# A hybrid decoder step on one core: new owners for the four PSUM banks of its chunked recurrence

## The chip, the core and the metric

The kernel runs on one core of a Trainium2 chip. The metric is device time in microseconds (us) of one execution; the figure to beat is the median of three timed runs. Engines are called PE or TensorE (matmul; PEld is its weight load), DVE or VectorE, ACT or ScalarE, POOL or GpSimd, and SP, whose queue issues most of the DMAs.

## What is computed

One inference step of a two-layer decoder trunk in float32, for a prompt of 1024 positions and for 8 sample sequences of 8 positions that share the weights. Layer 0 has a Conformer convolution mixer, layer 1 an RWKV-7 time mixer; each layer then has cross-attention to 256 memory tokens and a squared-ReLU MLP. The part that the change touches is the recurrence of layer 1, 16 heads with a 64 x 64 state each:

```python
def step(s, inp):
    rt, wt, kt, vt, at, bt = inp
    sa = jnp.einsum('bhvk,bhk->bhv', s, at)
    s = s * wt[:, :, None, :] + sa[..., None] * bt[:, :, None, :] + vt[..., None] * kt[:, :, None, :]
    yt = jnp.einsum('bhvk,bhk->bhv', s, rt)
    return s, yt
...
y, s = wkv7_scan(rh, decay, kh, vh, -kk, kk * ah, s0)
y = standardize(y, LNX_EPS).reshape(bsz, t, d) * lnx_g + lnx_b
y = (y + bonus.reshape(bsz, t, d)).astype(h.dtype)
out = (y * g) @ rw_w_o
```

## The kernel before

The positions are cut into two parts. Stream A works on part 0 (512 prompt positions), stream B on part 1 (512 prompt positions and the 64 sample positions). Each stream goes through all stages of both layers. A planner (`pace`) interleaves the two in program order: each stage is a generator that yields planned microseconds, and the stream whose planned clock is behind goes next. From that program order, with priorities, a scheduler at build time fixes the order on every engine and queue and puts in the semaphore waits; on the chip each engine and queue works strictly in its fixed order. The scan has its priority raised by 1000 places (`SCAN_AHEAD`).

Large products are made of three matmuls on high and low parts (lines 142 to 144); each weight tile is loaded to a raw buffer (four of them, line 120), cast on ScalarE (line 96) and split on VectorE or GpSimd (line 97).

The recurrence (`scan`) works on chunks of 64 positions, 8 columns of 128 partitions (two heads in each). Stream A scans chunks 0 to 7 beside B's projections; B then scans the samples (chunk `None`) and chunks 8 to 15 beside A's output projection, attention and MLP of layer 1. Projections leave r, k, v, the decay, a and g of every position in a DRAM scratch, in slots 0 to 5. Of a chunk three generators exist, and `together` gives each a turn in rotation, for three neighbouring chunks at once:

- `prep` loads five slots into `ld` (one buffer; eight DMAs at line 1146) and works on them elementwise (lines 1159 to 1196, `ar` and `bk` on GpSimd at 1183 to 1192); then products: sums (1201), the pair products of `ar` and `bk` (1217) with masks into `at`, `Aak`, `Aq` (1220 to 1222), v transposed into `UV` (1228, 1230), `bk` transposed into `BK` (1238), `AV` (1244, 1246), and last the bonus `bon`, which reads v in `ld` (1249, 1251).
- `inverse` inverts the chunk's triangular matrices: small blocks on VectorE, then four hops on TensorE (1320, 1326, 1335, 1345), each followed by an evacuation.
- `rest` has `step` and `finish`. `step` is the recurrence itself: `pz` from the state S (1374), y's part from S (1378), Z (1381), U (1386) and its two copies into `UV` (1387, 1388), the state's product (1393) and y's part from `UV` (1396), and the new S (1398, 1399). `finish` copies y (1488) and normalises it: sum (1445), centred y (1446), square (1449), sum (1450), Ln (1452), Exp (1453), five GpSimd instructions, and the store.

The scan has four of the eight PSUM banks; the other stream has the other four. In the kernel before they are called `pp` (two buffers in rotation), `pz` and `py`:

| bank | who uses it, for each chunk |
|---|---|
| `pp`, two | ten turns of `prep`, four hops of `inverse` (tag `iv`), U of `step` |
| `pz` | the two products of `step` that are added to `AV` and to S |
| `py` | y from its first product to its copy, then both norm sums |

Of the kernel before, what the change touches and what calls it, by code (L numbers as in the profile page):

```python
# [171 lines left out]
def body(tc, nc, es, a, o):  # L172
# [556 lines left out]
    def projections(s, ctx, part, h):  # L729
# [136 lines left out]
        def project(slot, after, *sides):  # L866


            for m0, k in ((0, 2), (2, 1), (3, 1), (4, 1), (5, 1), (6, 2)):
                wts = weights.take(k)  # L870
                for tt in tiles:
                    t0, n = tt
                    for m, wt in enumerate(wts, m0):
                        ps = s.bank()
                        s.prod(ps[:, :n], wide(wt, h, tt))
                        t = s.small("st")
                        nc.scalar.copy(t[:, :n], ps[:, :n])
                        store(t, m, slot, t0, n)
                        yield cost(n)
                        for side in sides:  # L880
                            yield next(side, 0)
                    if m0 == 6 and after is not None:
                        yield from mix(after, tt)
# [200 lines left out]
PE_PAIRS = (4, 3)  # L1084
BUF = dict(w=5, bon=2, at=2, ar=2, Aq=2, UV=2, AV=2, BK=2, pcs=3)


def scan(tc, nc, a, o, s, ph, kept, env):
# [9 lines left out]
    def bank(tag):  # L1098
        if tag == "iv":
            tag = "pp"  # L1100
        return sps.tile([P, 512], F32, tag=tag, name="p_" + tag, bufs=2 if tag == "pp" else 1)

    bones = con_tile(cn, "bones")
# [28 lines left out]
    def v3(t):  # L1132
        return t.rearrange("p (c t) -> p c t", c=8)
# [14 lines left out]
    def prep(chunk):  # L1148

        sam = chunk is None  # L1150
        kind = "_s" if sam else "_p"
        ld = new([P, 5, 512], "ld")
        load(ld, chunk, slice(0, 5))
        r, k, v, ws, ag = (ld[:, i] for i in range(5))
        ar = new([P, 8, 2, 64], "ar")
# [104 lines left out]
    def invert(at, tt, deep):  # L1260
# [48 lines left out]
        def iv():  # L1309
            return bank("iv")[:, :256].rearrange("p (i t) -> p i t", i=8)  # L1310

# [55 lines left out]

    def step(w, py, S):

        UV = w["UV"]  # L1370
        pz = v3(bank("pz"))
        for i in range(8):
            for h, s in heads:
                nc.tensor.matmul(pz[s, i], lhsT=w["ar"][s, i, 0], rhs=S[s, i], start=True, stop=True)

        for i in range(8):
            for h, s in heads:
                nc.tensor.matmul(py[s, i * 64:i * 64 + 64], lhsT=S[s, i], rhs=w["ar"][s, i, 1], start=(i == 0),
                                 stop=False)
        Z = new([P, 8, 64], "Z8")  # L1380
        nc.vector.tensor_add(Z, pz, w["AV"])
        yield
        pu = v3(bank("pp"))
        for i in range(8):
            for h, s in heads:
                nc.tensor.matmul(pu[s, i], lhsT=w["tt"][s, i], rhs=Z[s, i], start=True, stop=True)
        nc.vector.tensor_copy(UV[:64, :, 0], pu[:64])
        nc.scalar.copy(UV[:64, :, 1], pu[64:])
        yield
        pz = v3(bank("pz"))  # L1390
        for i in range(8):
            for h, s in heads:
                nc.tensor.matmul(pz[s, i], lhsT=w["BK"][:, i, h], rhs=UV[:, i, h], start=True, stop=True)
        for i in range(8):
            for h, s in heads:
                nc.tensor.matmul(py[s, i * 64:i * 64 + 64], lhsT=UV[:, i, h], rhs=w["Aq"][:, i, h], start=False,
                                 stop=(i == 7))
        nc.vector.tensor_add(S, pz, S)
        nc.vector.tensor_tensor(S, S, w["pcs"].unsqueeze(2).broadcast_to([P, 8, 64]), MUL)

    def step_samples(w, y, q):
# [7 lines left out]

        py = bank("py").rearrange("p (c i t) -> p c i t", c=4, i=2)  # L1410
        for g, c in enumerate(range(8)[cs]):
# [30 lines left out]

    def finish(w, y, py):
        chunk = w["chunk"]
        nc.tensor.matmul(py, lhsT=bones, rhs=y, start=True, stop=True)
        nc.vector.scalar_tensor_tensor(out=y, in0=py, scalar=-1.0 / 64, in1=y, op0=MUL, op1=ADD)
        yield
        rs = w512("rs")
        nc.scalar.activation(rs, y, AF.Square, scale=1.0 / 8)
        nc.tensor.matmul(py, lhsT=bones, rhs=rs, start=True, stop=True)  # L1450
        yield
# [17 lines left out]
    def rest(w):  # L1469

        chunk = w["chunk"]
        y = w512("y")
        if chunk is None:
            for i in range(2):
                yield from step_samples(w, y, i)
                yield
            py = bank("py")
        else:
            py = bank("py")
            if chunk == 0:  # L1480
                state[0] = states.tile([P, 8, 64], F32, tag="S", name="S")
                nc.gpsimd.memset(state[0], 0.0)
            S = state[0]
            yield from step(w, py, S)
            yield
            if chunk == 15:
                nc.sync.dma_start(out=o["wkv_p"].rearrange("m p v -> p m v"), in_=S)
            nc.scalar.copy(y, py)
        yield
        yield from finish(w, y, py)  # L1490
        yield
# [179 lines left out]
```

## Time and profile before

| | |
|---|---|
| timed runs | median 3887.41 us of 3 (3883.94 to 3888.81) |
| the profiled execution | 3875.96 us, span 3874.2 us, mean granted clock 0.955 |
| TensorE busy | 3627.8 us, 94% of the span |
| VectorE, ScalarE, GpSimd busy | 61%, 42%, 17% |
| scan of stream A | about 1740 to 2215 us of the span |
| scan of stream B | about 2375 to 2940 us of the span |

The profile has one execution. Busy times are unions of an engine's instructions. In a list of waits, "PE X <- DVE Y" says that TensorE stood idle before X until VectorE ended Y. The clock of TensorE is given as a share of full speed. A float32 matmul of this kernel shows as two rows of the trace, so 16 matmuls are x32. A row with "<-issue" has no releaser that the profile shows.

### The profile page before, as it was taken

To read this page: it belongs to the slowest core of one execution; us is meant where nothing else is said; L and a number is where in the kernel's file an instruction comes from. 1 tells how busy PE (TensorE), PEld (TensorE's weight loads), DVE (VectorE), ACT (ScalarE), POOL (GpSimd) and SP (SyncE) were. 2 spreads that over 40 slices of the span, in tenths; PEclk is the share of its full clock that TensorE was granted. 3 is DMA by queue.
4 is the path that set the end of the run, shared out by engine and by line. 5 is a ranking of instruction groups with operands and counts; after the bars stand their busy time and mean duration, and the time that the engine had idled before them with its cause. 6 is when DMAs were issued, how large, how long until landed. Compare 5 with 4: busy or idle time off the path is not lost. (4 is left out here: it accounts for less than half of the span.)

```text
span 3874.2 us, 75595 instructions
## 1 busy us (share of the span) xinstructions
PE 3627.8 (94%) x30906; PEld 3366.4 (87%) x30906; DVE 2353.9 (61%) x4479; ACT 1616.1 (42%) x3180; POOL 656.7 (17%) x704
## 2 busy tenths in 40 slices
PE   8989979999999999999899888979899999989998
PEld 7767769999999999999678688757789999989998
DVE  7889974646554653438767526587875536563334
ACT  3223253445433454443556634344444336432222
POOL 0010031024101100012221200232222015101110
PEclk9989989999999999999799899879899999999998
DMA  6424223335422344453245385323224336422221
GB/s 223 131 58 127 81 63 111 99 123 175 146 87 85 124 157 157 156 147 91 83 140 152 93 272 158 98 67 82 67 75 142 112 103 193 144 77 82 82 82 63
DMA packets 330827, 456.01 MB, mean 118 GB/s; under 512 B 153072, under 2 KB 245488, under 8 KB 330480
## 3 DMA queue, kind: packets, MB, share of 16 engines
q1 hardware_dynamic: 302832, 424.42, 35.9%
q10 hardware_dynamic: 27648, 26.75, 2.0%
q8 instruction: 243, 3.98, 0.4%
q14 instruction: 104, 0.85, 0.1%
HBM read 369.11 MB, written 73.49 MB: 114 GB/s over the span
## 5 line engine op out<-in xcount | busy, mean ns | idle before, releaser
L97 DVE TENSOR_TENSOR wt<-raw,wt 128x1024 fp32r<-128x1024 f32 x447 | 569.6, 1277 | 490.2 <-ACT wt L96 483.2
L96 ACT CAST wt<-raw 128x1024 fp32r<-128x1024 f32 x488 | 508.2, 1046 | 489.3 <-PE B_d L144 254.0
L142 PE MATMUL B_d<-hAB,wt 128*128 128x288 f32 (+1 forms) x2240 | 671.1, 302 | 12.6 <-ACT wt L96 5.2
L142 PE MATMUL A_d<-hAA,wt 128*128 128x256 f32 x2240 | 639.2, 288 | 32.8 <-ACT wt L96 16.7
L143 PE MATMUL B_d<-hBB,wt 128*128 128x288 f32 (+1 forms) x2240 | 668.5, 299 | 0.2
L144 PE MATMUL B_d<-hAB,wt 128*128 128x288 f32 (+1 forms) x2240 | 664.8, 298 | 0.5 <-DVE wt L97 0.3
L143 PE MATMUL A_d<-hBA,wt 128*128 128x256 f32 x2240 | 640.1, 287 | 4.2 <-DVE hBA L97 4.1
L144 PE MATMUL A_d<-hAA,wt 128*128 128x256 f32 x2240 | 632.5, 285 | 4.8 <-DVE wt L97 2.6
L142 PEld LDWEIGHTS A_d<-hAA,wt 128*128 128x128 f32 x2240 | 428.6, 192 | 49.5 <-ACT wt L96 20.9
L142 PEld LDWEIGHTS B_d<-hAB,wt 128*128 128x128 f32 x2240 | 424.1, 190 | 22.3 <-ACT hAB L96 7.5
L143 PEld LDWEIGHTS A_d<-hBA,wt 128*128 128x128 f32 x2240 | 429.9, 192 | 14.1 <-DVE hBA L97 5.9
L144 PEld LDWEIGHTS A_d<-hAA,wt 128*128 128x128 f32 x2240 | 427.7, 192 | 10.7 <-DVE wt L97 3.4
L143 PEld LDWEIGHTS B_d<-hBB,wt 128*128 128x128 f32 x2240 | 425.8, 190 | 5.2 <-DVE hBB L97 1.5
L144 PEld LDWEIGHTS B_d<-hAB,wt 128*128 128x128 f32 x2240 | 425.3, 190 | 3.2 <-issue 1.7
L711 POOL TENSOR_TENSOR t_sg<-t_ev 128x256 f32<-128x256 f32 (+1 forms) x256 | 185.0, 723 | 1427.8 <-ACT t_ev L709 1329.9
L142 PE MATMUL B_d<-u,wt 128*128 128x288 f32 x1024 | 304.2, 299 | 0.0
L144 PE MATMUL B_d<-u,wt 128*128 128x288 f32 x1024 | 302.2, 298 | 0.0
L143 PE MATMUL B_d<-u,wt 128*128 128x288 f32 x1024 | 302.1, 297 | 0.0
L143 PE MATMUL A_d<-u,wt 128*128 128x256 f32 x1024 | 288.8, 282 | 3.7 <-DVE u L97 3.7
L144 PE MATMUL A_d<-u,wt 128*128 128x256 f32 x1024 | 289.6, 283 | 0.0
L142 PE MATMUL A_d<-u,wt 128*128 128x256 f32 x1024 | 288.3, 283 | 0.0
L97 DVE TENSOR_TENSOR u<-t_sg,u 128x256 fp32r<-128x256 f32 (+1 forms) x256 | 133.2, 521 | 152.5 <-ACT u L96 152.1
(403 smaller groups left out, 7064.3 us busy)
## 6 DMA issues: line engine op xcount, KB each, us to landing
raw<-in_mlp_up_dram SPq DMA_DIRECT2D x128, 512.0 KB, 3.6
raw<-in_mlp_dn_dram SPq DMA_DIRECT2D x128, 512.0 KB, 3.6
raw<-in_rw_w_dram SPq DMA_DIRECT2D x64, 512.0 KB, 4.3
ld<-scr SPq DMA_DIRECT2D x136, 160.0 KB, 3.9
wf<-in_w_in_dram SPq DMA_DIRECT2D x32, 512.0 KB, 3.9
raw<-in_xa_w_q_dram SPq DMA_DIRECT2D x32, 512.0 KB, 3.6
raw<-in_xa_w_o_dram SPq DMA_DIRECT2D x32, 512.0 KB, 3.5
raw<-in_ck_dram SPq DMA_DIRECT2D x32, 512.0 KB, 3.6
```

Of the source, the lines that this page charges most:

```text
L96: self.nc.scalar.copy(hi, src)
L97: (engine or self.nc.vector).tensor_tensor(lo, src, hi.bitcast(F32), SUB)
L142: self.nc.tensor.matmul(out, lhsT=wh, rhs=mh, start=(i == 0), stop=False)
L143: self.nc.tensor.matmul(out, lhsT=wh, rhs=ml, start=False, stop=False)
L144: self.nc.tensor.matmul(out, lhsT=wl, rhs=mh, start=False, stop=(i == last))
L711: nc.gpsimd.tensor_mul(sg[:, :n], r[:, :n], r[:, :n])
```

## The change

Of the scan's four banks, `pp` (two buffers) keeps only the tiles of a chunk's own `prep` (and those of the samples). U of `step` and the two norm sums of `finish` go to `pz`. The fourth bank becomes one tile, `shared`, that is never given back; a function `half` hands out its two halves of 256 columns in turn, to the four hops of the inverse and to y. y is therefore made in two halves: for each, its products with S and with `UV` follow each other and ScalarE copies it out. Both halves now stand between U and the state's product, and `step` has one yield less. The projections store r, k, v to slots 1, 2, 0, so that `ld` holds slots 1 to 4 and v is loaded into a tile of its own with two buffers, by eight more DMAs a chunk.

```diff
--- before.py
+++ after.py
@@ -875,7 +875,7 @@
                         s.prod(ps[:, :n], wide(wt, h, tt))
                         t = s.small("st")
                         nc.scalar.copy(t[:, :n], ps[:, :n])
-                        store(t, m, slot, t0, n)
+                        store(t, m, (slot + 1) % 3, t0, n)
                         yield cost(n)
                         for side in sides:
                             yield next(side, 0)
@@ -1082,7 +1082,7 @@
 CONV_COST = 0.96
 TMP = dict(A=dict(acc=2, sq=2, rs=2, h=2, sg=2, ev=2, dl=2, st=2), B=dict(h=2, sg=2, ev=2, sq=2), Bp=dict(dl=2, st=2), Bm0=dict(sg=2))
 PE_PAIRS = (4, 3)
-BUF = dict(w=5, bon=2, at=2, ar=2, Aq=2, UV=2, AV=2, BK=2, pcs=3)
+BUF = dict(w=5, bon=2, at=2, ar=2, Aq=2, UV=2, AV=2, BK=2, v=2, pcs=3)
 
 
 def scan(tc, nc, a, o, s, ph, kept, env):
@@ -1096,9 +1096,14 @@
     wk = s.pool(ph, "swk")
 
     def bank(tag):
-        if tag == "iv":
-            tag = "pp"
         return sps.tile([P, 512], F32, tag=tag, name="p_" + tag, bufs=2 if tag == "pp" else 1)
+
+    shared, turns = bank("half"), [0]
+
+    def half():
+
+        turns[0] += 1
+        return shared[:, turns[0] % 2 * 256:turns[0] % 2 * 256 + 256]
 
     bones = con_tile(cn, "bones")
     masks = {n: con_tile(cn, n) for n in ("strict_p", "incl_p", "pair16", "sel", "sel32") +
@@ -1149,9 +1154,11 @@
 
         sam = chunk is None
         kind = "_s" if sam else "_p"
-        ld = new([P, 5, 512], "ld")
-        load(ld, chunk, slice(0, 5))
-        r, k, v, ws, ag = (ld[:, i] for i in range(5))
+        ld = new([P, 4, 512], "ld")
+        load(ld, chunk, slice(1, 5))
+        r, k, ws, ag = (ld[:, i] for i in range(4))
+        v = w512("v")
+        load(v, chunk, 0)
         ar = new([P, 8, 2, 64], "ar")
         bk = new([P, 8, 2, 64], "bk")
 
@@ -1307,7 +1314,7 @@
         td = td[:, :8]
 
         def iv():
-            return bank("iv")[:, :256].rearrange("p (i t) -> p i t", i=8)
+            return half().rearrange("p (i t) -> p i t", i=8)
 
         if deep:
 
@@ -1365,36 +1372,38 @@
         nc.scalar.copy(UV[:64, cs, 1], pz[64:, :, 64:128])
         yield
 
-    def step(w, py, S):
+    def step(w, y, S):
 
         UV = w["UV"]
         pz = v3(bank("pz"))
         for i in range(8):
             for h, s in heads:
                 nc.tensor.matmul(pz[s, i], lhsT=w["ar"][s, i, 0], rhs=S[s, i], start=True, stop=True)
-
-        for i in range(8):
-            for h, s in heads:
-                nc.tensor.matmul(py[s, i * 64:i * 64 + 64], lhsT=S[s, i], rhs=w["ar"][s, i, 1], start=(i == 0),
-                                 stop=False)
         Z = new([P, 8, 64], "Z8")
         nc.vector.tensor_add(Z, pz, w["AV"])
         yield
-        pu = v3(bank("pp"))
+        pu = v3(bank("pz"))
         for i in range(8):
             for h, s in heads:
                 nc.tensor.matmul(pu[s, i], lhsT=w["tt"][s, i], rhs=Z[s, i], start=True, stop=True)
         nc.vector.tensor_copy(UV[:64, :, 0], pu[:64])
         nc.scalar.copy(UV[:64, :, 1], pu[64:])
-        yield
+
+        for q in range(2):
+            py = half()
+            for i in range(4):
+                for h, s in heads:
+                    nc.tensor.matmul(py[s, i * 64:i * 64 + 64], lhsT=S[s, 4 * q + i], rhs=w["ar"][s, 4 * q + i, 1],
+                                     start=(i == 0), stop=False)
+            for i in range(4):
+                for h, s in heads:
+                    nc.tensor.matmul(py[s, i * 64:i * 64 + 64], lhsT=UV[:, 4 * q + i, h], rhs=w["Aq"][:, 4 * q + i, h],
+                                     start=False, stop=(i == 3))
+            nc.scalar.copy(y[:, 256 * q:256 * q + 256], py)
         pz = v3(bank("pz"))
         for i in range(8):
             for h, s in heads:
                 nc.tensor.matmul(pz[s, i], lhsT=w["BK"][:, i, h], rhs=UV[:, i, h], start=True, stop=True)
-        for i in range(8):
-            for h, s in heads:
-                nc.tensor.matmul(py[s, i * 64:i * 64 + 64], lhsT=UV[:, i, h], rhs=w["Aq"][:, i, h], start=False,
-                                 stop=(i == 7))
         nc.vector.tensor_add(S, pz, S)
         nc.vector.tensor_tensor(S, S, w["pcs"].unsqueeze(2).broadcast_to([P, 8, 64]), MUL)
 
@@ -1407,7 +1416,7 @@
             nc.sync.dma_start(out=t, in_=a["st_wkv"][:, c])
             S0.append(t)
 
-        py = bank("py").rearrange("p (c i t) -> p c i t", c=4, i=2)
+        py = bank("pp").rearrange("p (c i t) -> p c i t", c=4, i=2)
         for g, c in enumerate(range(8)[cs]):
             for b in range(NSEQ):
                 ts = slice(DSEQ * b, DSEQ * b + DSEQ)
@@ -1440,13 +1449,15 @@
                 nc.tensor.matmul(pu[s, g * 64:g * 64 + 64], lhsT=UV[:, c, h], rhs=w["Aq"][:, c, h], start=True, stop=True)
         nc.vector.tensor_add(y[:, 256 * q:256 * q + 256], y[:, 256 * q:256 * q + 256], pu[:, :256])
 
-    def finish(w, y, py):
+    def finish(w, y):
         chunk = w["chunk"]
+        py = bank("pz")
         nc.tensor.matmul(py, lhsT=bones, rhs=y, start=True, stop=True)
         nc.vector.scalar_tensor_tensor(out=y, in0=py, scalar=-1.0 / 64, in1=y, op0=MUL, op1=ADD)
         yield
         rs = w512("rs")
         nc.scalar.activation(rs, y, AF.Square, scale=1.0 / 8)
+        py = bank("pz")
         nc.tensor.matmul(py, lhsT=bones, rhs=rs, start=True, stop=True)
         yield
         nc.scalar.activation(rs, py, AF.Ln, bias=epsv)
@@ -1474,20 +1485,17 @@
             for i in range(2):
                 yield from step_samples(w, y, i)
                 yield
-            py = bank("py")
         else:
-            py = bank("py")
             if chunk == 0:
                 state[0] = states.tile([P, 8, 64], F32, tag="S", name="S")
                 nc.gpsimd.memset(state[0], 0.0)
             S = state[0]
-            yield from step(w, py, S)
+            yield from step(w, y, S)
             yield
             if chunk == 15:
                 nc.sync.dma_start(out=o["wkv_p"].rearrange("m p v -> p m v"), in_=S)
-            nc.scalar.copy(y, py)
         yield
-        yield from finish(w, y, py)
+        yield from finish(w, y)
         yield
 
     def together(*gens):
```

## Rows read from the trace of the kernel before

**Rows 1.** The page: busy time, share of the span and instructions of each engine.

```profile
PE 3627.8 (94%) x30906; PEld 3366.4 (87%) x30906; DVE 2353.9 (61%) x4479; ACT 1616.1 (42%) x3180; POOL 656.7 (17%) x704
```

**Rows 2.** Windows: length; busy PE, PEld, DVE, ACT, POOL (x instructions); clock, DMA share, GB/s.

```profile
1740.00:2215.00 475.00, 428.29 (x5153) 370.29 (x5151) 349.69 (x795) 269.95 (x547) 114.11 (x104) 0.91 0.41 115
1850.00:1950.00 100.00, 80.22 (x973) 64.82 (x974) 82.87 (x210) 55.44 (x120) 25.07 (x28) 0.74 0.40 110
2375.00:2940.00 565.00, 494.31 (x5994) 422.95 (x5994) 406.95 (x844) 247.23 (x489) 153.81 (x127) 0.89 0.31 84
2500.00:2650.00 150.00, 119.59 (x1286) 94.11 (x1282) 109.80 (x210) 64.82 (x131) 53.57 (x42) 0.83 0.27 71
2700.00:2750.00 50.00, 40.31 (x466) 32.56 (x464) 38.86 (x99) 23.29 (x46) 7.48 (x6) 0.81 0.26 69
2750.00:2800.00 50.00, 46.79 (x636) 41.97 (x635) 43.13 (x83) 25.29 (x60) 16.64 (x17) 0.95 0.29 70
3500.00:3600.00 100.00, 100.00 (x754) 100.00 (x754) 39.25 (x63) 28.14 (x47) 10.07 (x16) 1.00 0.27 80
```

**Rows 3.** Chain of waits, 2500 to 2940: shares by line, then pieces (start, us).

```profile
by line: PE A_d L143 8.8%; PE A_d L144 8.8%; PE A_d L142 8.7%; PE p_pp L1217 4.8%; SPq L1146 4.2%; DMA ld<-scr 3.5%; DVE wt L97 3.3%; issue 2.9%; DVE M L1297 2.3%; DVE ld L1164 2.1%; DVE w L1190 2.0%; DVE e L551 1.7%; DVE w L1196 1.6%; PE p
...
2555.73 0.68 DVE bon L1251
...
2561.56 3.78 DMA ld<-scr
...
2567.92 0.60 DVE w L1159
```

**Rows 4.** Timelines of TensorE and VectorE (start, us, engine, line; idle before and releaser).

```profile
2565.55 1.15 PE L1374 MATMUL p_pz<-S,ar 64*64 64x64 f32 x32 [0.93 <-DVE S L1399]
...
2573.19 1.19 PE L1378 MATMUL p_py<-ar,S 64*64 64x64 f32 x32 [2.14 <-ACT rs L1452]
...
2609.47 1.15 PE L1386 MATMUL p_pp<-Z,tt 64*64 64x64 f32 x32 [0.37 <-ACT AV L1246]
...
2612.09 0.67 DVE L1251 TENSOR_TENSOR bon<-ld,p_pp 128x512 f32<-128x512 f32 x1
```

**Rows 5.** Waits of TensorE in the whole span: total, times, longest.

```profile
PE p_pp L1320 <- DVE Aq L1222: 10.6, 6, 3.8
...
PE p_py L1378 <- ACT rs L1452: 7.7, 4, 2.7
...
PE p_py L1445 <- ACT y L1488: 4.9, 3, 4.0
```

**Rows 6.** Instructions on the y bank: duration ns min/median/max, first and last start.

```profile
L1488 ACT COPY y<-p_py x16: 581/587/588, 1832.7 to 2928.2; 128x512 f32<-128x512 f32 x16
...
L1418 ACT COPY y<-p_py x2: 378/378/378, 2448.9 to 2495.8; 128x256 f32<-128x256 f32 x2
```

**Rows 7.** Waits of ScalarE from 1740 to 2940.

```profile
ACT UV L1388 <- DVE UV L1387: 35.1, 15, 4.6
```

**Rows 8.** The queue of SP: the recurrence's loads; its waits, second and first scan.

```profile
L1146 SPq DMA_DIRECT2D gg<-scr x136: 319/432/2028, 1735.9 to 2926.2; - x136
...
SPq L1146 <- DVE bon L1251: 38.7, 5, 23.2
...
SPq L1146 <- DVE bon L1251: 23.4, 5, 13.1
```

**Rows 9.** Timeline of TensorE: two hops of the inverse and a prep's products.

```profile
2643.41 0.48 PE L1320 MATMUL p_pp<-T,dgz 32*32 32x16 f32 x34
2643.83 0.49 PE L1217 MATMUL p_pp<-ar,bk 64*128 64x128 f32 x2
...
2646.27 0.39 PE L143 MATMUL A_d<-hBA,wt 128*128 128x256 f32 x1
...
2649.05 0.93 PE L1217 MATMUL p_pp<-ar,bk 64*128 64x128 f32 x6
...
2650.48 0.71 PE L1326 MATMUL p_pp<-td,Y 32*32 32x16 f32 x62
```

## Prediction

> **What bounds the kernel now.** The page comes first: TensorE is busy 3627.8 of 3874.2 us [rows 1], so 246 us is all that better order could win, and the matmuls themselves don't change. The windows then say where those 246 us lie. From 3500 to 3600, as in most stretches without the scan, TensorE is busy throughout. The two scans stand in 1740 to 2215 and 2375 to 2940: there it idles 475.0 - 428.3 = 46.7 and 565.0 - 494.3 = 70.7 us, together 117.4, and its granted clock is 0.91 and 0.89, which costs about 428.3 x 0.09 + 494.3 x 0.11 = 92.9 us more [rows 2]. Idle time and clock go together: each us of idle has 0.79 us of lost clock beside it. After 2940 the engine is full, so a microsecond won inside the scans comes off the end.
>
> Three stretches hold half of the idle time: 1850 to 1950, 2500 to 2650 and 2700 to 2750. There the other stream has few matmuls ready (its norms and its attention), and the scan's own latency decides. They hold 19.8 + 30.4 + 9.7 = 59.9 us idle and about 20.9 + 20.3 + 7.7 = 48.9 us of clock [rows 2].
>
> What the scan's latency consists of is read from the chain of waits and the timeline. In the second scan the chain runs through the loads of `ld`: issue on SP 4.2% and landing 3.5% of 440 us, 33.9 us [rows 3]. The reader is to see why: `ld` has one buffer, its last reader is `bon` at the end of prep (it reads v), and only then may the next chunk's eight loads go out. From `bon` to the first use of the new `ld` pass 2567.92 - 2555.73 = 12.2 us. The second delay is the bank pair `pp`. The step's first product (L1374) runs at 2565.55, its second (L1386) at 2609.47, released by the evacuation of AV, just before `bon` at 2612.09 [rows 4]: it takes its turn in `pp` behind a whole prep, 43.9 us.
>
> **The change part by part.**
>
> *v in its own two tiles, the store slots rotated so that slots 1 to 4 are one slice.* `ld` is now free after its elementwise readers, before the prep's products, so the next load can go out while the present prep still runs. Gain: nothing at least, if what comes after is late anyway. At most the whole share of the chain, 33.9 us in the second scan. Four of its six loads in that stretch lie on the chain (4 x 3.8 us make the 3.5%), 5.65 us a round over six; over the seven later loads of the first scan, for which the chain has no rows, the same share would be 39.5 us. Upper end 73.4 us, below the 108.8 us that the three stretches hold. Which value? What is late next is VectorE: it is busy 82.9 + 109.8 + 38.9 = 231.5 of these 300 us, 77%, and in its fullest slice of this scan 43.13 of 50, 86.3% [rows 2]. If the starved stretches shrink until it is that full, they last 231.5 / 0.863 = 268 us: **-31.6 us**, idle and clock together. I take this; it lies near the middle of 0 and 73.4.
>
> The price is eight more issues a chunk on SP, 17 x 8 = 136 of about 0.432 us, as one-slot loads of gg take: 58.8 us of SP's queue. Queued behind them are the other stream's weight loads. Their cover is that SP now stands 38.7 + 23.4 = 62.1 us at the head of its queue waiting for `bon` [rows 8], with the same loads behind it; if that wait stays, some of 58.8 us would reach weights, and four raw buffers stand before TensorE. I cost it at nothing.
>
> *`pp` for a chunk's own tiles alone.* A round took 15 turns of `pp` (ten in prep, four hops, one step), now ten. The hops' wait for a prep's masks, 10.6 us in the trace, goes, and so does y's wait for the previous norm's Ln, 7.7 us [rows 5]. Both are pieces of the same idle time, so they are not added to the 31.6.
>
> *U and the two norm sums in `pz`.* The bank's order is now step, U, state, two norm sums, next step. U follows Z at once, about 40 us sooner. The next step's first product now waits for the previous Ln, where y's product did: in rows 4 that is 2573.19 instead of 2565.55, 7.6 us. At most that is 7.6 us a round; I take nothing, because the old step then stood 36 us before it went on. The first norm sum waits for the state's add as well as for y's copy; of this too the round has plenty.
>
> *y in halves.* All 32 products of y move between U and the state's product, eight of each half needing no UV: about 0.6 us of work that covers part of the UV copies. ScalarE copies 2 x 378 instead of 587 ns [rows 6], 16 x 0.169 = 2.7 us of an engine that is 42% busy [rows 1]. The new wait is the second half behind the copy of the first, if two halves of one bank exclude each other. The trace shows such a pair: ScalarE's copy of one half of U's partitions waits for VectorE's copy of the other half, 35.1 us in 15 times [rows 7]. Queued behind it on TensorE are the state's product and whatever of the other stream was ordered after. From below: nothing, if other matmuls were placed between. From above: the copy plus a busy ScalarE, as in y's wait before (4.9 us in 3, 1.6 each [rows 5]): 16 x 2.0 = 32 us. I take the bare copy, 16 x 0.378 = **+6.0 us**, because an order made for such waits mostly fills them.
>
> The Trainium skill, page "PSUM — Partial Sum Buffer", section "PSUM bank collisions raise a hardware error", speaks against this part: two engines must be kept apart by bank and quadrant and not by address, so two halves of a bank are one place. [...]
>
> *One yield fewer.* A round has 24 instead of 25 turns (10 prep, 8 inverse, 6 rest), so about 1.3 planned us of the other stream's work per chunk move behind the scan, where TensorE is full: moved, not saved. In a starved stretch it is 1.3 us less cover; nothing in the sum.
>
> Sum: -31.6 + 6.0 = -25.6 us. The profiled execution took 3875.96 us (span 3874.2), so 3850; it lies 11.5 us below the median of the timed runs, and carried over to them the forecast is 3887.4 - 25.6 = **3862 us**.
>
> **The rivals.**
>
> *VectorE already decides, or the load is no earlier in effect (no change).* For it: VectorE is at 77 to 86% where TensorE starves, and the chain passes through it between the loads [rows 2, 3]. SP works in order, so an `ld` freed early may still queue behind a weight load. Against it: 7.7% of the chain is load and nothing else. Time 3887, at most some us less.
>
> *y's second half blocks TensorE (slower).* The place is between the two halves, the price 16 x (0.378 + 1.6) = 32 us idle, with clock at 0.79 beside it 57 us; saved against that only the two waits of rows 5, 18.3 x 1.79 = 33 us. Net +24: 3912. It decides from about 1.1 us of stall per chunk on (18.3 / 16). Against it: another stream's matmuls can stand there.
>
> *Hops and products mix more finely.* With banks of their own, hops and a prep's products can be ready together, and switching between their shapes costs. At 2643.41 a hop's 64 rows with eight rows of L1217 between take until 2646.27, 2.86 us; apart they would be 0.73 (0.71 for 62 rows) and 1.24 (0.93 for six), so mixing costs 0.89 us [rows 9]. All 64 hops mixed are at most 57 us; half of them 28, which eats the gain: about 3890. Against it: they mix already. The Trainium skill, page "TensorEngine Tiling (Array Packing)", section "Key Properties", says that a change of tiling mode drains TensorE; the trace agrees, by the 0.89 us.
>
> **How the numbers follow.** Forecast 0.53 (alone: 3814 to 3880); no change 0.19; the blocked half 0.16; finer mixing 0.12. A measurement of this kernel tells about 0.2%, 7.8 us. Faster: 0.53, and 0.07 of the second and fourth case, 0.60. Slower: 0.16, and 0.07 from these two, 0.23. Same: 0.17. The range reaches from the whole share of the chain, 73.4 us less, to most of the blocked half: 3815 to 3905, with under 2 in 10 outside.
>
> **What would show it.** Right: loads of `ld` go out before `bon` and leave the chain; the wait of SP for `bon` is gone; L1386's successor follows Z within a few us; rounds there last clearly under the 56.4 us from one `bon` to the next (2555.73 to 2612.09, [rows 3, 4]); clock in the scan windows rises. y's second products show waits under 0.5 us. Wrong: the idle time in the scan windows stays near 117 us with VectorE over 85%; or y's second half shows over 1 us per chunk; or stretches of alternating hops and products are more frequent.

## The result, and the profile after

The changed kernel takes 3834.8 us (median of four runs, 3829.8 to 3837.4), the kernel before beside it 3885.8 (3883.9 to 3888.8). The ratio is 0.9867 [0.9849, 0.9884]: 51 us less, about twice the forecast 25.6. The time is inside the range; but, as the experiments show, the gain comes from another part of the change than the one forecast, and how large it is depends on the order that is built: in two other orders the same change gains 1.6% and 0.4%.

The two profiled executions differ less: spans of 3874.2 and 3835.7 us, 38.5 us. First the page of the kernel after, its busy times:

```profile
PE 3623.9 (94%) x30906; PEld 3369.6 (88%) x30906; DVE 2351.6 (61%) x4479; ACT 1610.0 (42%) x3190; POOL 660.7 (17%) x704
```

TensorE is busy 3.9 us less than in [rows 1]; 34.6 us of the difference is idle time that went. The windows say where (columns as in [rows 2]; the scans now stand in 1740 to 2130 and 2390 to 2850):

```profile
1740.00:2130.00 390.00, 349.76 (x4661) 300.09 (x4660) 314.93 (x700) 213.90 (x429) 116.85 (x105) 0.89 0.37 99
2130.00:2390.00 260.00, 240.34 (x1643) 224.56 (x1642) 107.17 (x236) 132.61 (x286) 9.01 (x13) 0.95 0.70 220
2390.00:2850.00 460.00, 415.08 (x5397) 348.05 (x5396) 360.83 (x746) 218.45 (x439) 153.17 (x118) 0.88 0.30 81
2543.00:2780.00 237.00, 214.69 (x3020) 180.29 (x3020) 209.01 (x461) 123.24 (x249) 86.35 (x65) 0.87 0.28 72
2850.00:3835.00 985.00, 955.01 (x7450) 949.14 (x7448) 485.26 (x861) 351.20 (x626) 150.64 (x186) 0.98 0.34 108
```

The scans last 850 us instead of 1040, but TensorE is also busy 157.8 us less in them (764.8 against 922.6): most of those 190 us are the other stream's matmuls, which now stand between and behind the scans. What was won is the idle time in them, 85.2 instead of 117.4. The clock there did not rise, though the prediction named that as a sign; it fell, from 0.91 and 0.89 to 0.89 and 0.88. VectorE is busy 209.0 of 237 us, 88%, over the rounds from 2543 to 2780.

The timeline of one round, by engine (SP's rows are issues; a row with x8 is the eight issues of a load):

```profile
2591.14 0.69 PE L1342 MATMUL p_half<-T,at 32*32 32x32 f32 x32
2592.80 0.69 PE L1352 MATMUL p_half<-td,W 32*32 32x32 f32 x32
2596.37 1.15 PE L1388 MATMUL p_pz<-Z,tt 64*64 64x64 f32 x32
...
2601.64 0.62 PE L1400 MATMUL p_half<-Aq,UV 128*64 128x64 f32 x13
...
2602.10 1.15 PE L1406 MATMUL p_pz<-UV,BK 128*64 128x64 f32 x31
...
2603.97 0.68 PE L1396 MATMUL p_half<-ar,S 64*64 64x64 f32 x16
2604.58 0.69 PE L1400 MATMUL p_half<-Aq,UV 128*64 128x64 f32 x16
2604.74 1.18 POOL L1190 TENSOR_TENSOR ar<-w,E 128x512 f32<-128x512 f32 x1 [19.97 <-PE p_half L1396]
2605.89 1.19 POOL L1198 TENSOR_TENSOR ar<-ld,E 128x512 f32<-128x512 f32 x1
2607.11 5.43 SPq L1151 DMA_DIRECT2D ld<-scr  x8
...
2616.61 0.33 PE L1381 MATMUL p_pz<-S,ar 64*64 64x64 f32 x2
...
2619.87 1.27 PE L1381 MATMUL p_pz<-S,ar 64*64 64x64 f32 x30
...
2630.14 0.67 DVE L1258 TENSOR_TENSOR bon<-v,p_pp 128x512 f32<-128x512 f32 x1
...
2630.42 0.69 PE L1352 MATMUL p_half<-td,W 32*32 32x32 f32 x32
...
2633.90 0.33 PE L1388 MATMUL p_pz<-Z,tt 64*64 64x64 f32 x2
...
2634.47 1.08 PE L1388 MATMUL p_pz<-Z,tt 64*64 64x64 f32 x29
...
2672.69 0.69 DVE L1258 TENSOR_TENSOR bon<-v,p_pp 128x512 f32<-128x512 f32 x1
```

Five things are to be seen. From this `bon` to the next pass 42.6 us, where it was 56.4 before. The loads of `ld` start at 2607.11, 23 us before that prep's `bon` (2630.14); in [rows 3] they came after it. What frees `ld` now is `ar` on GpSimd, which had stood 19.97 us until y's products of an earlier chunk let go of its buffer. U (L1388) starts 2.9 and 2.8 us after the end of the last hop (L1352) and 17.3 us behind the start of the step's first product (L1381, two rows at 2616.61 and the rest from 2619.87): it waits for its chunk's inverse. And the state's product (L1406) stands between the two halves of y, so the second half has something before it. The waits agree; first TensorE's in the whole span, then GpSimd's in both scans and SP's in the second:

```profile
PE p_pz L1455 <- DVE S L1407: 6.6, 4, 4.4
...
PE p_pp L1245 <- DVE Aq L1229: 5.8, 5, 2.2
...
PE p_half L1400 <- ACT UV L1390: 0.7, 2, 0.5
...
POOL ar L1190 <- PE p_half L1396: 141.9, 10, 25.4
...
SPq L1151 <- POOL ar L1198: 31.6, 4, 15.7
...
SPq L1151 <- DVE bon L1258: 9.2, 3, 5.7
```

SP's wait for `bon` fell from 38.7 us [rows 8] to 9.2, and 31.6 us for `ar` took its place. No wait of y for the copy of its other half is listed. In the chain of the second scan the load has become shorter, not vanished: issue and landing are 2.4% and 1.9% of 2400 to 2850, where [rows 3] have 4.2% and 3.5%. Two of the places:

```profile
2605.93 1.17 POOL ar L1198
2610.82 4.31 DMA ld<-scr
...
2685.95 1.63 POOL ar L1198
2691.30 4.30 DMA ld<-scr
```

### The profile page after: what moved, and what is told of

The parts are those of the page before. It is cut to its first block, busy times and chain, and to the rows that moved or that the text cites. A ratio compares the mean times of both kernels' runs of the same rounds, so it can differ in the third digit from the quotient of the medians.

```text
span 3835.7 us, 75763 instructions
## 1 busy us (share of the span) xinstructions
PE 3623.9 (94%) x30906; PEld 3369.6 (88%) x30906; DVE 2351.6 (61%) x4479; ACT 1610.0 (42%) x3190; POOL 660.7 (17%) x704
## 4 chain that ended last, share of the span: by engine, by line
PE 77%; DVE 11%; ACT 4%; DMA 4%; issue 2%; POOL 1%; SPq 1%; ACTq 0%; DVEq 0%; POOLq 0%
PE B_d L142 11%; PE B_d L144 11%; PE B_d L143 11%; PE A_d L142 10%; PE A_d L143 9%; PE A_d L144 9%; PE A_d L362 3%; PE B_d L362 2%; DMA scr<-t_st 1%; SPq L1151 1%; PE A_hd L810 1%; PE A_d L442 1%; PE B_sa L608 1%; DVE wt L97 1%; PE B_sa L610 1%
## 5 line engine op out<-in xcount | busy, mean ns | idle before, releaser
L97 DVE TENSOR_TENSOR wt<-raw,wt 128x1024 fp32r<-128x1024 f32 x447 | 567.3, 1272 | 476.9 <-ACT wt L96 473.0
L142 PE MATMUL B_d<-hAB,wt 128*128 128x288 f32 (+1 forms) x2240 | 673.6, 303 | 15.4 <-ACT hAB L96 6.3
L142 PE MATMUL A_d<-hAA,wt 128*128 128x256 f32 x2240 | 639.1, 288 | 15.0 <-ACT hAA L96 13.6
L142 PEld LDWEIGHTS A_d<-hAA,wt 128*128 128x128 f32 x2240 | 429.0, 192 | 25.1 <-ACT hAA L96 16.8
L142 PEld LDWEIGHTS B_d<-hAB,wt 128*128 128x128 f32 x2240 | 425.4, 191 | 24.5 <-ACT hAB L96 7.5
L142 PE MATMUL B_d<-u,wt 128*128 128x288 f32 x1024 | 307.1, 301 | 0.0
L142 PE MATMUL A_d<-u,wt 128*128 128x256 f32 x1024 | 287.4, 282 | 0.0
```

The costliest lines, as they stand in the source:

```text
L97: (engine or self.nc.vector).tensor_tensor(lo, src, hi.bitcast(F32), SUB)
L142: self.nc.tensor.matmul(out, lhsT=wh, rhs=mh, start=(i == 0), stop=False)
```

## The experiments

Two theories stood against each other: that the earlier load of `ld` (v in its own tiles) shortens the scan and with it the time, and that the new owners of the banks do. A third took shape with the first results: that the built order of TensorE decides, above all how finely the hops are cut into other products.

**How a span is split.** For each run the trace gives three parts of the span: idle time of TensorE; lost clock, which is half of TensorE's busy time in stretches granted 1.2 GHz instead of 2.4; and the rest, work at full clock. The split is approximate, for small shapes above all: in the kernel after the median row of L142 takes 285 ns at the full clock and 415 at half, one of the first hop only 178 and 209, so half the clock does not cost half of every busy time. And it comes from one execution of each kernel, which lay up to 13 us from the median of its runs (after_less: 3824.9 and 3837.5); single differences of a few us are not to be read. "Cuts" counts the runs without interruption into which the 64 hops fall in TensorE's built order; 64 is uncut. Ratios are to the kernel before on the same chip, and their intervals reach 0.0009 to 0.0027 to either side.

| kernel | ratio | span | work | idle | lost clock | cuts |
|---|---|---|---|---|---|---|
| before | 1 | 3874.2 | 3505.1 | 246.5 | 122.7 | 154 |
| after | 0.9867 | 3835.7 | 3486.4 | 211.8 | 137.5 | 100 |
| v_alone | 1.0020 | 3886.8 | 3519.6 | 218.5 | 148.7 | 164 |
| banks_alone | 0.9854 | 3826.7 | 3486.3 | 215.3 | 125.0 | 116 |
| yield_back | 0.9947 | 3865.3 | 3481.5 | 231.2 | 152.6 | 109 |
| ar3 | 0.9997 | 3872.3 | 3494.6 | 224.3 | 153.4 | 101 |
| before_grouped | 0.9849 | 3817.0 | 3485.6 | 222.4 | 109.0 | 64 |
| v_grouped | 0.9971 | 3867.7 | 3497.5 | 217.3 | 152.9 | 65 |
| banks_grouped | 0.9839 | 3830.2 | 3480.7 | 229.3 | 120.2 | 64 |
| after_grouped | 0.9986 | 3880.2 | 3477.8 | 260.9 | 141.5 | 64 |
| hops_back | 0.9869 | 3828.5 | 3517.0 | 200.4 | 111.0 | 174 |
| u_back | 0.9932 | 3855.7 | 3490.2 | 213.5 | 152.0 | 100 |

**v_alone: v's own tiles, without the banks.** To the kernel before only this is done:

```diff
-                        store(t, m, slot, t0, n)
+                        store(t, m, (slot + 1) % 3, t0, n)
...
-BUF = dict(w=5, bon=2, at=2, ar=2, Aq=2, UV=2, AV=2, BK=2, pcs=3)
+BUF = dict(w=5, bon=2, at=2, ar=2, Aq=2, UV=2, AV=2, BK=2, v=2, pcs=3)
...
-        ld = new([P, 5, 512], "ld")
-        load(ld, chunk, slice(0, 5))
-        r, k, v, ws, ag = (ld[:, i] for i in range(5))
+        ld = new([P, 4, 512], "ld")
+        load(ld, chunk, slice(1, 5))
+        r, k, ws, ag = (ld[:, i] for i in range(4))
+        v = w512("v")
+        load(v, chunk, 0)
```

> The kernel before with the edit to v alone: slots rotated, ld of four slots, v in two tiles of its own; the banks, y and the yields as before. Theory ld (ld's early release carries the gain): 30 to 50 us faster than before, rounds of the second scan near 45 us. Theory banks (the turns of pp carry it): within 10 us of before, since U and the hops still take their turn in pp. Theory both (each frees one delay and the other then holds): each edit alone under half of the 51 us.

Measured: 3890.1 us, 1.0020 [1.0011, 1.0029]. The scan did become shorter: in its row for `bon` (duration min, median, max; first and last start) the last one starts 68 us sooner than in the kernel before, whose row stands first:

```profile
L1251 DVE TENSOR_TENSOR bon<-ld,p_pp x17: 673/679/695, 1771.3 to 2893.5; 128x512 f32<-128x512 f32 x17
...
L1253 DVE TENSOR_TENSOR bon<-v,p_pp x17: 674/680/705, 1773.8 to 2825.7; 128x512 f32<-128x512 f32 x17
```

The windows of its two scans:

```profile
1740.00:2150.00 410.00, 369.25 (x4602) 312.89 (x4601) 317.40 (x704) 214.70 (x429) 104.86 (x102) 0.89 0.36 99
2375.00:2940.00 565.00, 503.66 (x5819) 424.24 (x5818) 406.67 (x846) 248.49 (x495) 152.63 (x133) 0.85 0.32 89
```

SP's wait for `bon` in both scans falls from 62.1 us [rows 8] to 17.2. TensorE idles 28.0 us less in the whole span, where the prediction had 31.6 for idle time and clock together; but it has 14.5 us more work and 26.0 us more lost clock (0.85 in the window of the second scan, where [rows 2] have 0.89), and the time does not fall. The first theory falls here: the load was late, it is early now, and it is worth nothing.

**banks_alone: the banks, without v's own tiles.** The three edits of v_alone are undone in the kernel after. "The banks" thus stand for all the rest of the change, y in halves and the missing yield included.

> The changed kernel with ld as before: five slots in one tile, v read from it, the old slots; banks, halves of y and yields as in the changed kernel. Theory ld: within 12 us of before, the chain of waits still goes through the loads of ld. Theory banks: 30 to 50 us faster than before. Theory both: under 25 us faster.

Measured: 3828.4 us, 0.9854 [0.9839, 0.9869], the whole gain. Its scan ends as early as that of v_alone, by its row for `bon`:

```profile
L1256 DVE TENSOR_TENSOR bon<-ld,p_pp x17: 670/682/689, 1774.3 to 2823.8; 128x512 f32<-128x512 f32 x17
```

and yet its loads still wait for `bon`, as SP's waits in the second scan show (38.7 in [rows 8]), and their issue and landing are still 4.2% and 4.7% of the chain from 2400 to 2850:

```profile
SPq L1151 <- DVE bon L1256: 48.0, 5, 14.8
```

Two kernels with the same length of scan, one at 1.002 and one at 0.985: the scan's length is not what sets the time.

**yield_back.** In the kernel after, the removed yield is put back.

```diff
         nc.scalar.copy(UV[:64, :, 1], pu[64:])
+        yield
```

> The changed kernel with the yield after the copies of U put back, so that a round has 25 turns again. Theory ld and theory banks: within 8 us of the changed kernel. A theory of pace (the gain comes from 1.3 planned us less of the other stream per round): it loses 15 us or more of the 51.

Measured: 3864.0 us, 0.9947 [0.9934, 0.9961], 29 us more than the kernel after. Work at full clock is about the same (3481.5 and 3486.4 us); idle time and lost clock grow by 19.4 and 15.1. That is the loss that the theory of pace asked for; but it may be the yield itself or only the other order that comes with it, and the runs with other planned costs below bear on that.

**ar3.** The kernel after waits for `ar`'s two buffers; here they are three, and v has one.

```diff
-ar=2, Aq=2, UV=2, AV=2, BK=2, v=2, pcs=3
+ar=3, Aq=2, UV=2, AV=2, BK=2, v=1, pcs=3
```

> The changed kernel with three buffers of ar (and one of v, to make room). In the profile after, GpSimd's first write of ar waits 141.9 us in 10 times for y's products, which read the buffer two chunks back, and SP's load of ld stands behind that write. If this is the delay that is late next: 10 to 30 us faster than the changed kernel, rounds of the second scan under 38 us. If VectorE (80% busy in the scans after) decides by now: within 8 us of the changed kernel.

Measured: 3883.8 us, 0.9997 [0.9984, 1.0010]: the gain is gone. GpSimd's wait fell, as meant, from 141.9 us to 56.1; its row in both scans:

```profile
POOL ar L1190 <- PE p_half L1396: 56.1, 4, 18.1
```

But the loads did not go out sooner: SP's loads now wait for `bk` on GpSimd, 68.8 us in both scans, and 25.5 us for `bon`, where in the kernel after it was 49.7 us for `ar` and 23.3 for `bon`:

```profile
SPq L1151 <- POOL bk L1199: 68.8, 13, 13.8
```

So the run does not tell whether the wait for `ar` limits the kernel after, and whether v's single tile took back the gain was not separated.

**The grouped kernels: each of the four kernels with its hops kept together.** The matmuls of each hop are raised in priority, so that no other product is ordered between them.

```diff
-            for i in range(8):
+            with tc.high_priority(200):
+                for i in range(8):
...
```

(the same at the other three hops; in this way for before, v_alone, banks_alone and after)

> The kernel before with one edit: the matmuls of each of the four hops get a higher priority at build time, so that a hop goes out as one run (64 runs of hops in TensorE's order instead of 154). Theory mixing (in the kernel before, hops cut into a prep's products cost time, and the banks' change wins by untangling them): 15 to 30 us faster than before, busy time of the pair products down from 76 us towards 64. Theory pp turns (the waits for a bank are what cost): within 8 us of before.

> The edit to v alone, with each hop as one run. Theory mixing (v alone gained 28 us of idle time and lost it to 164 runs of hops, pair products busy 96 us): 25 to 45 us faster than v alone, so 20 to 40 us faster than before. Otherwise within 8 us of v alone, 3890 us.

> The edit to the banks alone, with each hop as one run (64 instead of 116). Theory mixing: 5 to 15 us faster than the banks alone, 3828 us. Otherwise within 6 us of it.

> The changed kernel with each hop as one run (64 instead of 100). Theory mixing: 5 to 12 us faster than the changed kernel, 3835 us. Otherwise within 6 us of it.

Measured: 0.9849 [0.9834, 0.9864], 0.9971 [0.9959, 0.9982], 0.9839 [0.9826, 0.9853] and 0.9986 [0.9977, 0.9995]. The kernel before gains 57 us by this alone, as much as by the whole change (the intervals overlap); v_alone gains 18 us, less than expected; banks_alone gains 6; and the kernel after loses 44, which no theory expected. Its timeline shows what [rows 9] did not, hops that run through at once:

```profile
2612.74 0.73 PE L1321 MATMUL p_pp<-T,dgz 32*32 32x16 f32 x64
2613.40 1.16 PE L1217 MATMUL p_pp<-ar,bk 64*128 64x128 f32 x8
...
2618.76 0.73 PE L1328 MATMUL p_pp<-td,Y 32*32 32x16 f32 x64
2623.01 0.69 PE L1338 MATMUL p_pp<-T,at 32*32 32x32 f32 x32
```

The first hop takes 0.73 us, the price that the prediction worked out for a hop apart. Work at full clock falls by 19.5 us in before and by 22.1 in v_alone, which were cut most, and by 5.6 and 8.6 in the other two. That finer cutting costs work is thus shown; but the hops are not all that is cut. In v_grouped the hops run through (65 runs), and still the pair products are busy for 93.4 us: there the products of y with `UV` are ordered between them, row by row.

```profile
2641.20 0.33 PE L1402 MATMUL p_py<-Aq,UV 128*64 128x64 f32 x2
2641.45 0.49 PE L1219 MATMUL p_pp<-ar,bk 64*128 64x128 f32 x2
2641.87 0.33 PE L1402 MATMUL p_py<-Aq,UV 128*64 128x64 f32 x2
...
L1219 PE MATMUL p_pp<-ar,bk 64*128 64x128 f32 x544 | 93.4, 329 | 4.9 <-DVE d L1207 2.5 <-POOL bk L1194 1.1 <-DVE Aq L1224 1.1
```

A better count than the cuts is how often the shape (`32*32`, `64*128` and so on in the rows) changes from one TensorE row to the next: 1287 times in before, 1392 in v_alone, 1226 in banks_alone, 1199 in after, 1136 in before_grouped. Over all 20 kernels (1133 to 1481 changes) work rises with it, by a fit of 0.17 us a change, with a correlation of 0.97; with the cuts it is 0.86.

Work is not the whole time, as the last of the four shows. After_grouped has the least work of the table and is 44 us slower than after: its idle time is 49 us longer, and the windows put it into the two scans (62.7 and 71.2 us idle, where the kernel after has 40.2 and 44.9):

```profile
1740.00:2130.00 390.00, 327.34 (x4527) 277.11 (x4526) 304.94 (x658) 191.61 (x383) 118.30 (x106) 0.88 0.34 90
...
2390.00:2850.00 460.00, 388.83 (x4895) 328.60 (x4894) 369.42 (x776) 218.39 (x451) 138.74 (x111) 0.85 0.33 88
```

VectorE is about as full there (304.9 and 369.4 us, against 314.9 and 360.8). Why the grouping leaves that time idle stays open.

**hops_back and u_back: one owner undone.** In the kernel after, the hops go back to `pp`; or U does.

```diff
         def iv():
-            return half().rearrange("p (i t) -> p i t", i=8)
+            return bank("pp")[:, :256].rearrange("p (i t) -> p i t", i=8)
```

> The changed kernel with the four hops back in pp (y's halves keep their bank). In the order that is built, TensorE gets 174 runs of hops instead of 100 (before: 154). Theory mixing: 25 to 50 us slower than the changed kernel, pair products busy over 75 us. Theory U (U's own bank is what wins): within 10 us of the changed kernel.

```diff
-        pu = v3(bank("pz"))
+        pu = v3(bank("pp"))
```

> The changed kernel with U back in pp. 100 runs of hops, as in the changed kernel. Theory mixing: within 10 us of the changed kernel. Theory U: 25 us slower or more, U again 7 to 10 us behind the end of its inverse.

Measured: hops_back 3830.9 us, 0.9869 [0.9854, 0.9884], where the theory of mixing asked for a loss; u_back 3858.4 us, 0.9932 [0.9905, 0.9959]. With the hops in `pp` again they are cut into 174 runs, and work at full clock rises by 30.6 us; yet the time stays, since idle time falls by 11.4 and lost clock by 26.5. So in this one order a bank of their own for the hops is not needed for the gain, and fine cutting does not have to cost time. U in `pp` costs 24 us, but not by the delay that its theory named: U comes 0.5 to 5.6 us behind the last hop of its inverse, as in the kernel after (1.2 to 5.5), and not 7 to 10. Of the 20.0 us between the spans 14.5 are lost clock, 3.8 work and 1.7 idle time.

**The same four kernels in two other orders.** One edit changes the built order of everything near it, and the differences above are as small as that may be worth. So the 2 x 2 (neither, v alone, banks alone, both) was built with two other planned costs of the scan, 3% lower and 3% higher; the instructions are the same.

```diff
-SCAN_COST = [1.344, 1.248]
+SCAN_COST = [1.304, 1.211]
```

(less; for more, [1.384, 1.285])

> The kernel before with the scan's planned costs at 0.97 of theirs (1.304 and 1.211), an edit that changes no instruction, only the order at build time: a measure of what an order alone is worth. Theory mixing: 186 runs of hops instead of 154, so 5 to 20 us slower than before. If the order's other parts swing by more than the mixing: over 15 us to either side, against the count.

> The changed kernel with the scan's planned costs at 0.97 of theirs, again the order alone: 106 runs of hops instead of 100. Theory mixing: within 8 us of the changed kernel. If the order's other parts swing as they did with the yield put back (29 us): over 12 us slower.

> The edit to v alone, planned costs of the scan at 0.97: the same instructions in another order, 190 runs of hops. Theory banks (the banks carry the gain, v none, whatever the order): 3880 to 3915 us, as the kernel before in its orders. Theory luck (v alone and the banks alone differ by their orders): the gap of 62 us between them closes to under 30.

> The edit to v alone, planned costs of the scan at 1.03, 194 runs of hops. Theory banks: 3880 to 3915 us. Theory luck: anywhere from 3830 on.

> The edit to the banks alone, planned costs at 0.97, 103 runs of hops. Theory banks: 3815 to 3850 us, 40 us or more below v alone in the same order. Theory luck: up to 3880.

> The edit to the banks alone, planned costs at 1.03, 92 runs of hops. Theory banks: 3815 to 3850 us. Theory luck: up to 3880.

> The kernel before, planned costs at 1.03, 158 runs of hops. Theory banks: 3870 to 3900 us. Theory luck: from 3840 on.

> The changed kernel, planned costs at 1.03, 131 runs of hops. Theory banks: 3825 to 3860 us, at least 25 us below the kernel before in the same order. Theory luck: up to 3885.

| ratio to before | less | as built | more | mean |
|---|---|---|---|---|
| neither | 1.0040 | 1 | 0.9968 | 1.0003 |
| v alone | 1.0024 | 1.0020 | 1.0076 | 1.0040 |
| banks alone | 0.9880 | 0.9854 | 0.9844 | 0.9859 |
| both | 0.9884 | 0.9867 | 0.9928 | 0.9893 |

In every order the banks gain (1.2 to 1.6% without v's tiles, 1.4 to 1.5% with them), and v's own tiles do not: alone they change the time by -0.2, +0.2 and +1.1%, on top of the banks by +0.0, +0.1 and +0.8%. The whole change, from neither to both, gains 1.6, 1.3 and 0.4%, 1.1% in the mean; with the third costs that is 16 us, not the 25 or more that were expected, since before_more is faster (3866.3 us) than its range and v's tiles cost most there. The planned cost alone moves a kernel by 0.4 to 0.7% between its best and worst order. So single edits of about that size, U's 0.65% and the yield's 0.8%, are not attributed: each was seen in one order. So was the grouping, whose four results reach from -1.5 to +1.2%. The parts of the span, as means over the three orders:

| us | span | work | idle | lost clock | cuts | changes of shape |
|---|---|---|---|---|---|---|
| neither | 3877.8 | 3506.3 | 237.8 | 133.7 | 154 to 186 | 1287 to 1336 |
| v alone | 3896.1 | 3529.1 | 202.3 | 164.7 | 164 to 194 | 1392 to 1481 |
| banks alone | 3825.6 | 3479.7 | 221.5 | 124.4 | 92 to 116 | 1170 to 1226 |
| both | 3835.3 | 3492.1 | 213.7 | 129.5 | 100 to 131 | 1199 to 1272 |

Of the banks' 52.2 us, 26.6 are work, 16.3 idle time, 9.3 lost clock. v's tiles alone save more idle time than the banks (35.5 us), and lose it to work (+22.8) and clock (+31.0).

The fastest kernels of the study leave v in `ld`: banks_more (3819.8 us, 0.9844 [0.9828, 0.9860]), banks_grouped (3822.5, 0.9839) and before_grouped (3826.9, 0.9849). Their intervals touch or overlap that of the changed kernel, so that they beat the kernel before is shown, that they beat the changed one is not.

## Why the prediction was right, and where it was wrong

The direction was right and the time inside the range. The sum was not: its only gain, 31.6 us, is not where the gain came from, and the part that made it stands in the sum at nothing.

- **"-31.6 us", the term for v in its own tiles.** This step failed. Its mechanism was there (in v_alone SP's wait for `bon` falls from 62.1 to 17.2 us, and idle time by 28.0), but not its worth: by itself the part gives 1.0020, and over three orders 1.0040 against 1.0003. What failed is the use of 0.79 us of lost clock for each us of idle time, and the sentence "the matmuls themselves don't change". In v_alone idle time falls by 28.0 us, and lost clock and work rise by 40.5.
- **`pp` for a chunk's own tiles, "not added", U and norms "nothing".** This is where the gain is, together with the two small parts below that banks_alone also holds: 1.4% over three orders, 52 us of span. The prediction saw in it only the two waits of [rows 5], pieces of the same idle time. So the forecast that the time falls came true by a part to which it gave nothing, and that is luck. That U would follow Z some 40 us sooner is wrong. The last hop of that chunk's inverse, in the kernel before:

```profile
2601.45 1.06 PE L1345 MATMUL p_pp<-td,W 32*32 32x32 f32 x32 [0.88 <-ACT W L1339]
```

  37 of the 43.9 us lay before the end of this hop, and U came 7.0 us after it, not the whole prep that the prediction saw in front of it. Over both scans, without the first and last chunk of each, U came 4.6 to 11.3 us after that hop before and comes 1.2 to 5.5 after it now. Its distance from the step's first product was 36 to 55 us and is 9 to 34; most of that is the first product, which stands later in a shorter round.
- **The rival "hops and products mix more finely".** Its price for a hop that runs through was right (0.73 us), its sign was not: where they share `pp` with the prep the hops are cut into 154 to 194 runs, with half a bank of their own into 92 to 131. The pair products of L1217 (x544) are busy for less time too; first the row of before_grouped, then that of after:

```profile
L1217 PE MATMUL p_pp<-ar,bk 64*128 64x128 f32 x544 | 66.4, 315 | 11.2 <-POOL bk L1192 9.7 <-DVE Aq L1222 1.1 <-DVE d L1272 0.5
```

```profile
L1224 PE MATMUL p_pp<-ar,bk 64*128 64x128 f32 x544 | 63.6, 308 | 6.5 <-DVE Aq L1229 2.7 <-POOL ar L1198 1.6 <-POOL bk L1199 1.0
```

  Before they were busy 76.3 us, in v_alone 96.0; but the 93.4 of v_grouped show that there it is y's products and not the hops that cut them, a mixing that the rival did not name. Work at full clock is 3504.6 to 3535.3 us in the seven kernels with over 150 cuts and 3475.4 to 3499.0 in the thirteen with fewer. The Trainium skill, page "TensorEngine Tiling (Array Packing)", section "Key Properties", says that a change of tiling mode drains TensorE; the runs agree, by the 0.17 us of work with each change of shape. But hops_back, cut into 174 runs and as fast as the kernel after, shows that this work alone does not decide.
- **"+6.0 us" for y in halves.** In the kernel after next to nothing of it is seen. The second half never starts before the copy of the first has ended, in three of 16 rounds 0.05 us after it; but the state's product and the other stream's work stand between (2602.10 to 2603.97), and TensorE is idle before those starts for 0.3 us in all. The sentence "an order made for such waits mostly fills them" held for the copy itself too, in this order. In hops_back the wait is there, twice:

```profile
PE p_half L1396 <- ACT y L1402: 5.5, 2, 5.1
```

  The rival that the half blocks did not occur. The 35.1 us of [rows 7] were no evidence for it: the two copies of U read different partitions (`pu[:64]` and `pu[64:]`) and write one tile, so their wait tells nothing about two halves of a bank's columns.
- **SP's 136 issues at nothing:** nothing against it; ScalarE's waits for raw weights from 1740 to 2940 are 18.6 us before, 3.2 in v_alone and 16.8 after. No run separates the issues from the rest of v's tiles.
- **The yield at nothing:** the one run against it costs 29 us, about what an order alone moves; it was seen in one order and stays open, and with it how much of the banks' gain is the yield's.
- **VectorE fills up** to 88% in the rounds of the second scan, where the prediction stopped at 86.3%. That bound held about; it bounds the rounds, not the time. In v_alone, too, the rounds became shorter and the time did not.

What stays open: which of the banks' parts makes the gain (the norm sums and y in halves were never undone, U and the yield in one order alone); why the banks save work and idle time together when hops_back has the time without the work; why lost clock moves between 109 and 182 us among kernels of the same matmuls; why grouping the hops helps before and harms after.

## What to carry to other kernels

Where a full engine follows a starved stage, a shorter stage only moves work: read the whole span as work, idle time and lost clock, and expect a cut in one to come back in the others. When tiles of different shapes share a bank or a rotation, look at how finely their matmuls are cut into each other; holding one group together gave here as much as a new plan of the banks, and took it away again on top of that plan. And when an edit changes an order made at build time, try it in several orders before a difference of about 1% is put down to the edit: the same change was worth 0.4% here in one order and 1.6% in another.

## What the runs showed of the hardware

Lost clock did not follow idle time: from before to v_more (ratio 1.0076) idle time fell from 246.5 to 192.2 us and lost clock rose from 122.7 to 181.8. And the same 544 rows of pair products were busy for 61.8 us in after_grouped and 96.0 in v_alone, by what stood between them and by the clock. TensorE's work at full clock rose by about 0.17 us with each change of shape in its order, over 20 kernels with 1133 to 1481 changes.
